# Attention scores from 64-row products in both halves of the array, four heads to a softmax step

## The chip, the cores and the metric

One core of a Trainium2 chip runs the whole program. The metric is the device time of one execution in microseconds. Five engines take their own instruction queues: TensorE (PE, and PEld for its loads of weights), VectorE (DVE), ScalarE (ACT), GpSimd (POOL) and SyncE (SP), which only issues DMAs here.

## The reference

Two networks run one after the other on 256 rows of 1024 features. The first is a block with stick-breaking attention, a recurrence and a feed-forward part. The second has two layers of attention and a product-key expert layer. The change is in the attention of the second, and each layer computes there, with h the running activations:

```python
proj = h @ w_in[l]                      # 8 + 8 query heads, 2 + 2 key/value heads, 64 wide
qa = apply_axial_rope(rms_norm_2(qa, qn_g[l]), cos, sin)
ka = apply_axial_rope(rms_norm_2(ka, kn_g[l]), cos, sin)
oa = global_attention(qa, ka, va)       # softmax(q k / 8) v, 4 query heads to a key head
ob = window_sink_attention(qb, kb, vb, sink[l], slopes)
oa = rms_norm_2(oa, gn_a_g[l]...)       # each head by itself
ob = rms_norm_2(ob, gn_b_g[l]...)
mix = concat([oa, ob]) @ w_o[l]
h = layer_norm(ALPHA * h + mix, ln1_g[l], ln1_b[l])
h = layer_norm(ALPHA * h + peer_ffn(h, ...), ln2_g[l], ln2_b[l])
```

The windowed heads subtract a slope times the distance from the scores, leave out keys more than 128 away, and add a learned sink to the softmax's denominator. Everything is in fp32.

## The kernel before

`body` runs the first block, then for each of two layers `attention` and `peer`. All of it is written with a tile framework whose planner decides the order on each engine: it takes instructions by their place in the program, with those marked as high priority first, and by a timeline that it computes for itself. Engines take their instructions in that fixed order and wait for semaphores. Tiles of one tag share a given number of buffers, and a new tile waits until an old one was read for the last time. PSUM has eight banks of 512 fp32 columns in each partition.

`attention` first projects the input, in products of split fp32 weights, into queries and keys. The second key head of each kind stands in partitions 64 to 127 and the first in 0 to 63, and so do the queries that go with them: `qT[which][:, j]` holds head j of either key head, one in each half of the partitions. `which` is 0 for the global heads and 1 for the windowed ones. The keys `KB[which]` have 2 x 256 columns: 256 for each key head, with zeros in the other head's partitions (lines 1165 to 1168, filled by lines 1189 and 1220). So one product of 128 rows and 512 columns gives the scores of two heads at once (line 1239). In fp32 each product runs as two passes, and each pass is an own record of a weight load and a matmul.

The steps that follow run over 16 combinations in a layer: two halves t of the rows (128 queries each), two kinds `which`, four j; a step has two heads. In `attend` (line 1236) a step makes its scores in PSUM (`s`, three buffers of a bank), adds the slopes by two bf16 products for windowed heads (1241), takes the minimum of the negated scores (1245) and for windowed heads the sink (1248), then two exponentials on ScalarE that also sum (1250), corrects and inverts the sum (1252 to 1255), transposes the weights in four 128 x 128 pieces (1259) into the one buffer `pt`, copies them to SBUF (VectorE for global heads, 1264, ScalarE for windowed ones, 1262), multiplies by the values into the one buffer `o` (1268) and scales (1269). After each second step `norm` (1272) normalizes the four heads of a pair of j: a square, a sum, GpSimd's power (line 173), three products, and `transpose_split` (lines 371 to 373) through the one buffer `tr`. `out` (1295) multiplies them with the output weights (1304), into two banks that collect a half t. `load` (1292) brings these weights in during the first eight steps: ScalarE rounds them (221) and GpSimd subtracts (222). The loop over n at line 1319 sets the order: a step's norm comes one step after its pair is complete, its products with the output weights two steps after.

When the last product of a half is there, `residual` and `finish` (1307, 1311) add, normalize the rows and transpose them into `X`, which `peer` needs for its first product. `K.warm` fills the wait with products that nobody reads, in a buffer of `s`. PSUM in this stage: two banks for `out`, three for `s`, one each for `pt`, `o` and `tr`. `peer` takes over all but the first two. Weights stream in through three buffers `raw`, so DMAs for the next stage start when a buffer is free.

Of the kernel before, what the change touches and what calls it, by code (L numbers as in the profile page):

```python
# [8 lines left out]
F = mybir.dt.float32  # L9
# [10 lines left out]
S = 256  # L20
# [1099 lines left out]
def attention(tc, A, K, dump, h, l, X, B):  # L1120
# [5 lines left out]
    with ExitStack() as es:  # L1126
# [38 lines left out]
        KB = [at.tile([128, 2, S], F, name=f"KB{i}") for i in range(2)]  # L1165
        for x in KB:
            G.memset(x[64:128, 0], 0.0)
            G.memset(x[0:64, 1], 0.0)
# [15 lines left out]
        def evb(j, ps):  # L1184
            if j < 4:
                V.tensor_scalar_mul(qT[1][:, j], ps, -0.125)
            else:
                for kv in range(2):
                    SC.activation(KB[1][64 * kv:64 * kv + 64, kv], ps[64 * kv:64 * kv + 64], AF.Copy)

# [25 lines left out]
        for t in range(2):  # L1216
            w = K.bank()
            PE.transpose(w[:, 0:128], RP[:, t, 4].rearrange("p k d -> p (k d)"), ident)
            for kv in range(2):
                SC.activation(KB[0][64 * kv:64 * kv + 64, kv, ts(t)], w[64 * kv:64 * kv + 64, 0:128], AF.Copy)  # L1220
            w = K.bank()
            for j in range(4):
                PE.transpose(w[:, j * 128:(j + 1) * 128], RP[:, t, j].rearrange("p k d -> p (k d)"), ident)
            V.tensor_scalar_mul(qT[0][:, :, ts(t)], w.rearrange("p (j t) -> p j t", t=128), -0.125)
# [11 lines left out]
        def attend(which, t, j):  # L1236

            s = pb.tile([128, 2, S], F, name="s", tag="s", bufs=3)
            PE.matmul(s, lhsT=qT[which][:, j, ts(t)], rhs=KB[which], start=True, stop=not which)
            for kv in range(2 * which):  # L1240
                PE.matmul(s[:, kv], lhsT=slope[:, j + 4 * kv], rhs=db[:, t], start=False, stop=kv == 1)
            mn = at.tile([128, 2], F, name="mn", tag="mn", bufs=4)
            dn = at.tile([128, 2], F, name="dn", tag="dn", bufs=4)
            P = at.tile([128, 2, S], F, name="P", tag="P", bufs=3)
            V.tensor_reduce(mn, s, AX.X, OP.min)
            sk = nsink.rearrange("p (k j) -> p k j", k=2)[:, :, j]
            if which:
                V.tensor_tensor(mn, mn, sk, op=OP.min)
            for kv in range(2):
                SC.activation(P[:, kv], s[:, kv], AF.Exp, scale=-1.0, bias=mn[:, kv:kv + 1], accum_out=dn[:, kv:kv + 1])  # L1250
            if which:
                V.tensor_sub(mn, mn, sk)
                SC.activation(mn, mn, AF.Exp)
                V.tensor_add(dn, dn, mn)
            V.reciprocal(dn, dn)
            w = pb.tile([128, 512], F, name="pt", tag="pt").rearrange("p (a t) -> p a t", t=128)
            for kv in range(2):
                for i in range(2):
                    PE.transpose(w[:, 2 * kv + i], P[:, kv, ts(i)], ident)
            PT = at.tile([128, 4, 128], F, name="PT", tag="PT", bufs=2)  # L1260
            if which:
                SC.activation(PT, w, AF.Copy)
            else:
                V.tensor_copy(PT, w)
            o = pb.tile([128, 512], F, name="o", tag="o")
            for kv in range(2):
                for i in range(2):
                    PE.matmul(o[:, kv * 64:kv * 64 + 64], lhsT=PT[:, 2 * kv + i], rhs=VA[:, i, which, 64 * kv:64 * kv + 64], start=i == 0, stop=i == 1)  # L1268
            V.tensor_mul(O[:, t, 8 * which:8 * which + 8].rearrange("p (k j) d -> p k j d", k=2)[:, :, j],
                         o[:, 0:128].rearrange("p (k x) -> p k x", x=64), dn.unsqueeze(2).to_broadcast([128, 2, 64]))  # L1270

        def norm(which, t, a):
# [14 lines left out]
            K.transpose_split(lambda: pb.tile([128, 512], F, name="tr", tag="tr"), sq, OH[:, ks, ts(t)], OL[:, ks, ts(t)])  # L1287
# [23 lines left out]
        def finish(t):  # L1311
            K.layer_norm(h, t, lambda c: g1[:, c], lambda c: b1[:, c])
            K.transpose_split(K.bank if t else lambda: pb.tile([128, 512], F, name="tr", tag="tr"), h[:, t].rearrange("p (m k) -> p k m", k=8),
                              *[x[:, :, ts(t)] for x in X])

        X = K.xt()
        steps = [(which, t, j) for t in range(2) for which in range(2) for j in range(4)]
        order = [0, 2, 1, 3, 4, 6, 5, 7]
        for n in range(19):
            if n < 16:  # L1320
                attend(*steps[n])
                if n < 8:
                    load(order[n])
            if n > 1 and n % 2 == 0 and n <= 16:
                which, t, j = steps[n - 1]
                norm(which, t, j // 2)
            if n > 2 and n % 2 == 1 and n <= 17:
                which, t, j = steps[n - 2]
                out(which, t, j // 2)
                if n == 9:  # L1330
                    residual(0)
        w = pb.tile([128, 512], F, name="s", tag="s", bufs=3)[:, :S]
# [321 lines left out]
```

## Time and profile before

| | us |
|---|---|
| median of 3 runs (2461.76 to 2466.64) | 2463.34 |
| the profiled execution | 2460.61 |
| its span | 2458.8 |

| engine | busy, share of the span | instructions |
|---|---|---|
| PE | 95% | 17012 |
| DVE | 69% | 3190 |
| ACT | 49% | 2118 |
| POOL | 15% | 299 |

The mean granted TensorE clock is 0.982 of full speed. Busy times are shares over stages with different limits, and matmuls overlap in the records, so a stage has to be looked at by itself: by its windows, its chain of waits and its groups of instructions. In the chain, each piece is what the next one waited for or followed on its engine.

### The profile page before, as it was taken

To read this page: it belongs to the slowest core of one execution; us is meant where nothing else is said; L and a number is where in the kernel's file an instruction comes from. 1 tells how busy PE (TensorE), PEld (TensorE's weight loads), DVE (VectorE), ACT (ScalarE), POOL (GpSimd) and SP (SyncE) were. 2 spreads that over 40 slices of the span, in tenths; PEclk is the share of its full clock that TensorE was granted. 3 is DMA by queue.
4 is the path that set the end of the run, shared out by engine and by line. 5 is a ranking of instruction groups with operands and counts; after the bars stand their busy time and mean duration, and the time that the engine had idled before them with its cause. 6 is when DMAs were issued, how large, how long until landed. Compare 5 with 4: busy or idle time off the path is not lost.

```text
span 2458.8 us, 43487 instructions
## 1 busy us (share of the span) xinstructions
PE 2346.7 (95%) x17012; PEld 2122.6 (86%) x17012; DVE 1697.5 (69%) x3190; ACT 1205.5 (49%) x2118; POOL 370.3 (15%) x299
## 2 busy tenths in 40 slices
PE   8978989998999999999999999999999999999998
PEld 7877879977799999999888877689999999888886
DVE  4467565557789968886555556779967888556555
ACT  4663554444435445544545454534545554455543
POOL 0065400007304410000000004502430000000000
PEclk9999999998999999999999999999999999999999
DMA  5332146555145454545556565325455555566664
GB/s 176 86 108 76 57 145 185 185 181 164 57 138 164 155 179 157 166 161 188 191 196 191 194 204 179 112 78 168 152 171 165 163 163 178 190 191 196 192 194 146
DMA packets 145637, 389.68 MB, mean 158 GB/s; under 512 B 18731, under 2 KB 49510, under 8 KB 145174
## 3 DMA queue, kind: packets, MB, share of 16 engines
q1 hardware_dynamic: 140070, 375.34, 47.8%
q10 hardware_dynamic: 5360, 11.56, 1.5%
q8 instruction: 133, 2.18, 0.4%
q14 instruction: 74, 0.61, 0.1%
HBM read 385.34 MB, written 1.31 MB: 157 GB/s over the span
## 4 chain that ended last, share of the span: by engine, by line
PE 56%; DVE 14%; issue 2%; ACT 2%; DMA 2%; POOL 0%; ACTq 0%; DVEq 0%; POOLq 0%
PE w L1571 27%; PE a L1387 7%; PE a L1388 7%; PE a L1390 7%; DVE lo L222 3%; PE w L1542 2%; PE a L1304 2%; DVE s L1434 1%; DMA raw<-in_peer_v_dram 1%; DVE oh L1469 1%; ACT hi L221 1%; PE w L1423 1%; PE o L1268 1%; DVE oh L1472 1%; DVE ix L1436 1%
## 5 line engine op out<-in xcount | busy, mean ns | idle before, releaser
L221 ACT ACTIVATE hi<-raw 128x1024 fp32r<-128x1024 f32 (+1 forms) x696 | 709.2, 1023 | 853.1 <-PE w L1571 312.0
L222 DVE TENSOR_TENSOR lo<-raw,hi 128x1024 fp32r<-128x1024 f32 (+1 forms) x610 | 745.7, 1224 | 524.6 <-ACT hi L221 518.9
L1387 PE MATMUL a<-XH,hi 128*128 128x256 f32 x2048 | 505.8, 285 | 8.9 <-ACT S L1393 5.9
L1388 PE MATMUL a<-XL,hi 128*128 128x256 f32 x2048 | 499.9, 282 | 0.0
L1571 PE MATMUL w<-hi,ww 128*128 128x512 f32 x1968 | 488.9, 389 | 4.1 <-ACT ww L226 4.1
L1571 PEld LDWEIGHTS w<-hi,ww 128*128 128x128 f32 x1968 | 368.8, 188 | 83.0 <-ACT ww L226 6.6
L1387 PEld LDWEIGHTS a<-XH,hi 128*128 128x128 f32 x2048 | 391.3, 191 | 12.7 <-ACT S L1393 6.3
L1388 PEld LDWEIGHTS a<-XL,hi 128*128 128x128 f32 x2048 | 391.3, 191 | 0.0
L1390 PE MATMUL a<-XH,lo 128*128 128x256 f32 x2048 | 293.2, 284 | 8.3 <-DVE lo L222 8.3
L1390 PEld LDWEIGHTS a<-XH,lo 128*128 128x128 f32 x2048 | 262.8, 190 | 9.3 <-DVE lo L222 9.1
L1571 PE MATMUL w<-lo,ww 128*128 128x512 f32 x984 | 264.4, 390 | 0.0
L222 POOL TENSOR_TENSOR lo<-raw,hi 128x1024 fp32r<-128x1024 f32 (+1 forms) x86 | 190.6, 2226 | 314.0 <-ACT hi L221 289.1
L173 POOL TENSOR_TENSOR ag<-ag,mhalf 128x1 f32<-128x1 f32 x10 | 9.5, 951 | 1464.0 <-DVE ag L349 1253.0
L1571 PEld LDWEIGHTS w<-lo,ww 128*128 128x128 f32 x984 | 184.2, 188 | 40.3 <-DVE lo L222 2.3
L264 PE MATMUL pj<-XH,hi 128*128 128x256 f32 (+1 forms) x424 | 124.6, 299 | 5.1 <-ACT gs L593 3.3
L266 PE MATMUL pj<-XH,lo 128*128 128x256 f32 (+1 forms) x424 | 117.5, 300 | 4.9 <-DVE lo L222 3.8
L265 PE MATMUL pj<-XL,hi 128*128 128x256 f32 (+1 forms) x424 | 122.1, 293 | 0.0
L227 DVE TENSOR_TENSOR ww<-S,ww 128x256 fp32r<-128x256 f32 x246 | 102.5, 417 | 0.0
L226 ACT ACTIVATE ww<-S 128x256 fp32r<-128x256 f32 x246 | 98.0, 399 | 0.0
L265 PE MATMUL pj<-big,hi 128*128 128x256 f32 x352 | 97.8, 283 | 0.0
L264 PE MATMUL pj<-big,hi 128*128 128x256 f32 x352 | 97.4, 283 | 0.0
L266 PE MATMUL pj<-big,lo 128*128 128x256 f32 x352 | 92.6, 283 | 0.0
(502 smaller groups left out, 3564.3 us busy)
## 6 DMA issues: line engine op xcount, KB each, us to landing
raw<-in_peer_u_dram SPq DMA_DIRECT2D x256, 512.0 KB
raw<-in_peer_v_dram SPq DMA_DIRECT2D x256, 512.0 KB
raw<-in_w_in_dram SPq DMA_DIRECT2D x58, 512.0 KB
raw<-in_w_ffn_in_dram SPq DMA_DIRECT2D x88, 256.0 KB
raw<-in_peer_wq_dram SPq DMA_DIRECT2D x32, 512.0 KB
raw<-in_w_ffn_out_dram SPq DMA_DIRECT2D x22, 512.0 KB
raw<-in_w_o_dram SPq DMA_DIRECT2D x16, 512.0 KB
raw<-in_w_out_dram SPq DMA_DIRECT2D x8, 512.0 KB
```

The costliest lines, as they stand in the source:

```text
L221: nc.scalar.activation(a, r, AF.Copy)
L222: (sub or nc.vector).tensor_sub(b, r, a.bitcast(F))
L226: self.nc.scalar.activation(hi, xf, AF.Copy)
L227: self.nc.vector.tensor_sub(lo, xf, hi.bitcast(F))
L264: PE.matmul(ps[j], lhsT=wh, rhs=xh(kk), start=kk == 0 and j % per == 0, stop=False)
L265: PE.matmul(ps[j], lhsT=wh, rhs=xl(kk), start=False, stop=False)
L266: PE.matmul(ps[j], lhsT=wl, rhs=xh(kk), start=False, stop=kk == KT - 1 and (j % per == per - 1 or j == len(subs) - 1))
L1304: K.marks["out"] = PE.matmul(po[t][c], lhsT=x[:, k, ts(t)], rhs=w[:, c * 512:(c + 1) * 512], start=f and not i and k == ks[0], stop=e and ...
L1387: PE.matmul(a, lhsT=hi[:, k], rhs=XH[:, k], start=k == 0, stop=False)
L1388: PE.matmul(a, lhsT=hi[:, k], rhs=XL[:, k], start=False, stop=False)
L1390: PE.matmul(a, lhsT=lo[:, k], rhs=XH[:, k], start=False, stop=k == 7)
L1571: K.marks["v"] = PE.matmul(acc[t][:, n], lhsT=x[:, ts(t)], rhs=v[:, n * 512:(n + 1) * 512], start=f, stop=e)
```

## The change

Keys lose their zeros: `KB[which]` has 256 columns, both key heads one above the other, and is filled by one copy in place of two. `attend` takes two j at once, four heads: four score products of 64 rows and 256 columns, each with the queries and keys of one half of the partitions, into a tile `s` of two banks (one for each key head) with two buffers. Minimum, sink, correction, inversion and scaling then work on four heads in one instruction; exponentials, transposes, copies and value products stay as many as they were. The copy of the transposed weights is VectorE's for the first j and ScalarE's for the second, whatever the kind of heads. `norm` and `finish` take their transposes from `pt`, and `tr` is gone. The loop has nine turns: `attend` of a pair, then `norm` and `out` of the pair before.

```diff
-        KB = [at.tile([128, 2, S], F, name=f"KB{i}") for i in range(2)]
-        for x in KB:
-            G.memset(x[64:128, 0], 0.0)
-            G.memset(x[0:64, 1], 0.0)
+        KB = [at.tile([128, S], F, name=f"KB{i}") for i in range(2)]
...
-                for kv in range(2):
-                    SC.activation(KB[1][64 * kv:64 * kv + 64, kv], ps[64 * kv:64 * kv + 64], AF.Copy)
+                SC.activation(KB[1], ps, AF.Copy)
...
-            for kv in range(2):
-                SC.activation(KB[0][64 * kv:64 * kv + 64, kv, ts(t)], w[64 * kv:64 * kv + 64, 0:128], AF.Copy)
+            SC.activation(KB[0][:, ts(t)], w[:, 0:128], AF.Copy)
...
-        def attend(which, t, j):
-
-            s = pb.tile([128, 2, S], F, name="s", tag="s", bufs=3)
-            PE.matmul(s, lhsT=qT[which][:, j, ts(t)], rhs=KB[which], start=True, stop=not which)
-            for kv in range(2 * which):
-                PE.matmul(s[:, kv], lhsT=slope[:, j + 4 * kv], rhs=db[:, t], start=False, stop=kv == 1)
...
-            P = at.tile([128, 2, S], F, name="P", tag="P", bufs=3)
+        def attend(which, t, a):
+
+
+            s = pb.tile([128, 2, 2, S], F, name="s", tag="s", bufs=2)
+            for j in range(2):
+                for kv in range(2):
+                    r = slice(64 * kv, 64 * kv + 64)
+                    PE.matmul(s[:, kv, j], lhsT=qT[which][r, 2 * a + j, ts(t)], rhs=KB[which][r], start=not j, stop=j == 1 and not which)
+            for j in range(2 * which):
+                for kv in range(2):
+                    PE.matmul(s[:, kv, j], lhsT=slope[:, 2 * a + j + 4 * kv], rhs=db[:, t], start=False, stop=j == 1)
...
+            P = at.tile([128, 2, 2, S], F, name="P", tag="P", bufs=2)
             V.tensor_reduce(mn, s, AX.X, OP.min)
...
-            PT = at.tile([128, 4, 128], F, name="PT", tag="PT", bufs=2)
-            if which:
-                SC.activation(PT, w, AF.Copy)
-            else:
-                V.tensor_copy(PT, w)
...
+            o = pb.tile([128, 512], F, name="o", tag="o")[:, 0:256].rearrange("p (k j d) -> p k j d", k=2, j=2)
+            for j in range(2):
+                w = pb.tile([128, 512], F, name="pt", tag="pt").rearrange("p (a t) -> p a t", t=128)
+                for kv in range(2):
+                    for i in range(2):
+                        PE.transpose(w[:, 2 * kv + i], P[:, kv, j, ts(i)], ident)
+                PT = at.tile([128, 4, 128], F, name="PT", tag="PT", bufs=2)
+                if j:
+                    SC.activation(PT, w, AF.Copy)
+                else:
+                    V.tensor_copy(PT, w)
+                for kv in range(2):
+                    for i in range(2):
+                        PE.matmul(o[:, kv, j], lhsT=PT[:, 2 * kv + i], rhs=VA[:, i, which, 64 * kv:64 * kv + 64], start=i == 0, stop=i == 1)
+            V.tensor_mul(O[:, t, 8 * which:8 * which + 8].rearrange("p (k j) d -> p k j d", k=2)[:, :, 2 * a:2 * a + 2],
+                         o, dn.unsqueeze(3).to_broadcast([128, 2, 2, 64]))
...
-            K.transpose_split(lambda: pb.tile([128, 512], F, name="tr", tag="tr"), sq, OH[:, ks, ts(t)], OL[:, ks, ts(t)])
+            K.transpose_split(lambda: pb.tile([128, 512], F, name="tr", tag="pt"), sq, OH[:, ks, ts(t)], OL[:, ks, ts(t)])
...
-        for n in range(19):
-            if n < 16:
+        for n in range(9):
+            if n < 8:
                 attend(*steps[n])
-                if n < 8:
-                    load(order[n])
-            if n > 1 and n % 2 == 0 and n <= 16:
-                which, t, j = steps[n - 1]
-                norm(which, t, j // 2)
-            if n > 2 and n % 2 == 1 and n <= 17:
-                which, t, j = steps[n - 2]
-                out(which, t, j // 2)
-                if n == 9:
+                if n < 4:
+                    load(order[2 * n])
+                    load(order[2 * n + 1])
+            if n:
+                norm(*steps[n - 1])
+                out(*steps[n - 1])
+                if n == 4:
                     residual(0)
```

## Rows read from the trace of the kernel before

**Rows 1.** The page's first part: busy us (share of the span) and instructions.

```profile
PE 2346.7 (95%) x17012; PEld 2122.6 (86%) x17012; DVE 1697.5 (69%) x3190; ACT 1205.5 (49%) x2118; POOL 370.3 (15%) x299
```

**Rows 2.** Windows view: start and end, length, each engine's busy us, granted clock, DMA.

```profile
606.00:675.00 69.00, 63.47 (x355) 47.02 (x356) 48.73 (x143) 36.59 (x112) 24.30 (x21) 1.00 0.21 70
614.70:628.00 13.30, 11.67 (x68) 7.50 (x67) 13.22 (x36) 11.71 (x35) 9.95 (x9) 1.00 0.47 156
...
1561.60:1573.20 11.60, 9.50 (x60) 6.36 (x58) 11.43 (x27) 9.12 (x26) 10.04 (x9) 1.00 0.53 171
```

**Rows 3.** Chain of waits in the first layer's stage: shares, then start, us, what.

```profile
by line: PE a L1304 27.1%; PE o L1268 13.4%; PE s L1239 10.4%; PE pt L1259 7.8%; DVE mn L1245 6.5%; DVE sq L1283 2.8%; DVE PT L1264 2.6%; PE tr L371 2.6%; DVE mn L1248 2.5%; issue 2.3%; DVE h L1309 1.9%; ACT L1250 1.9%; DVE bs L346 1.7%; DV
...
606.18 0.28 ACT KB L1220
...
606.55 1.11 PE s L1239 x2
...
607.68 0.70 DVE mn L1245
...
621.25 0.07 DVE dn L1254
...
629.57 0.86 PE s L1239 x2
```

**Rows 4.** Chain of waits in the second layer's stage.

```profile
by line: PE a L1304 26.9%; PE o L1268 11.6%; PE s L1239 8.6%; ACT P L1250 7.3%; PE pt L1259 5.8%; issue 3.6%; DVE mn L1245 3.6%; PE tr L371 3.1%; DVE dn L1254 2.9%; ACT big L221 2.2%; DVE sq L1283 2.2%; DVE h L1309 1.8%; ACT L1250 1.8%; DVE
...
1551.03 1.70 PE s L1239 x2
```

**Rows 5.** Groups by line and form, 606 to 675 us: busy us, mean ns, idle before.

```profile
L373 DVE TENSOR_TENSOR big<-tr,big 128x256 fp32r<-128x256 f32 x8 | 3.4, 421 | 3.2 <-ACT big L372 3.2
...
L372 ACT ACTIVATE big<-tr 128x256 fp32r<-128x256 f32 x8 | 3.1, 383 | 13.4 <-PE tr L371 13.4
L1248 DVE TENSOR_TENSOR mn<-mn,nsink 128x2 f32<-128x2 f32 x8 | 2.5, 315 | 0.1
...
L1252 DVE TENSOR_TENSOR mn<-mn,nsink 128x2 f32<-128x2 f32 x8 | 1.9, 238 | 0.6 <-ACT P L1250 0.5
```

**Rows 6.** TensorE in order of time, products of 64 columns in either half.

```profile
120.71 0.66 PE L559 MATMUL w<-a,VS 128*64 128x256 f32 x4
121.19 0.39 PE L560 MATMUL w<-a,VS 128*64 128x128 f32 x4
...
283.15 0.32 PE L952 MATMUL pm<-QT,UU 128*64 128x128 f32 x1
283.15 0.32 PE L951 MATMUL pm<-RT,VN 128*64 128x128 f32 x1
283.31 0.27 PE L952 MATMUL pm<-QT,UU 128*64 128x128 f32 x1
```

**Rows 7.** TensorE in order of time, products of 64 rows between full ones.

```profile
206.16 1.02 PE L743 MATMUL pj<-ART,KZ 128*128 128x256 f32 x4
207.11 0.49 PE L786 MATMUL pm<-D 64*128 64x128 f32 x2
207.44 0.38 PE L787 MATMUL pm<-D 64*128 64x128 f32 x2
...
207.88 0.22 PE L790 MATMUL pm<-ident,D 64*128 64x64 f32 x1
208.03 0.71 PE L730 MATMUL pj<-VN,Nt 128*128 128x128 f32 x4
```

**Rows 8.** Groups by line and form, 1551 to 1621 us.

```profile
L1254 DVE TENSOR_TENSOR dn<-dn,mn 128x2 f32<-128x2 f32 x8 | 3.0, 373 | 1.0 <-ACT mn L1253 1.0
L1252 DVE TENSOR_TENSOR mn<-mn,nsink 128x2 f32<-128x2 f32 x8 | 2.7, 336 | 0.5 <-ACT P L1250 0.4
...
L1248 DVE TENSOR_TENSOR mn<-mn,nsink 128x2 f32<-128x2 f32 x8 | 2.4, 294 | 0.1
```

**Rows 9.** GpSimd in order of time.

```profile
616.17 2.54 POOL L222 TENSOR_TENSOR keep<-raw,keep 128x512 fp32r<-128x512 f32 x2
```

More of the change, by code (lines that the diff above doesn't have):

```diff
@@ L1255, in attend @@
             V.reciprocal(dn, dn)
[L1256 to L1259, printed above, removed]
-            PT = at.tile([128, 4, 128], F, name="PT", tag="PT", bufs=2)
-            if which:
-                SC.activation(PT, w, AF.Copy)
-            else:
-                V.tensor_copy(PT, w)
[L1265 to L1270, printed above, removed]
+            o = pb.tile([128, 512], F, name="o", tag="o")[:, 0:256].rearrange("p (k j d) -> p k j d", k=2, j=2)
+            for j in range(2):
+                w = pb.tile([128, 512], F, name="pt", tag="pt").rearrange("p (a t) -> p a t", t=128)
[7 more added lines that the diff above has]
+                    V.tensor_copy(PT, w)
+                for kv in range(2):
+                    for i in range(2):
+                        PE.matmul(o[:, kv, j], lhsT=PT[:, 2 * kv + i], rhs=VA[:, i, which, 64 * kv:64 * kv + 64], start=i == 0, stop=i == 1)
+            V.tensor_mul(O[:, t, 8 * which:8 * which + 8].rearrange("p (k j) d -> p k j d", k=2)[:, :, 2 * a:2 * a + 2],
+                         o, dn.unsqueeze(3).to_broadcast([128, 2, 2, 64]))
         def norm(which, t, a):
@@ L1312, in finish @@
             K.layer_norm(h, t, lambda c: g1[:, c], lambda c: b1[:, c])
-            K.transpose_split(K.bank if t else lambda: pb.tile([128, 512], F, name="tr", tag="tr"), h[:, t].rearrange("p (m k) -> p k m", k=8),
+            K.transpose_split(K.bank if t else lambda: pb.tile([128, 512], F, name="tr", tag="pt"), h[:, t].rearrange("p (m k) -> p k m", k=8),
                               *[x[:, :, ts(t)] for x in X])
         X = K.xt()
-        steps = [(which, t, j) for t in range(2) for which in range(2) for j in range(4)]
+        steps = [(which, t, a) for t in range(2) for which in range(2) for a in range(2)]
         order = [0, 2, 1, 3, 4, 6, 5, 7]
-        for n in range(19):
-            if n < 16:
+        for n in range(9):
+            if n < 8:
                 attend(*steps[n])
-                if n < 8:
-                    load(order[n])
-            if n > 1 and n % 2 == 0 and n <= 16:
-                which, t, j = steps[n - 1]
-                norm(which, t, j // 2)
-            if n > 2 and n % 2 == 1 and n <= 17:
-                which, t, j = steps[n - 2]
-                out(which, t, j // 2)
-                if n == 9:
+                if n < 4:
[5 more added lines that the diff above has]
+                if n == 4:
                     residual(0)
-        w = pb.tile([128, 512], F, name="s", tag="s", bufs=3)[:, :S]
+        w = pb.tile([128, 2, 2, S], F, name="s", tag="s", bufs=2)[:, 0, 0]
         K.warm(48, "out", w)
```

9 lines of the change are left out of this document (4 added, 5 removed).

## The prediction

> **What bounds the kernel now.** I read the page's line of engine totals first: TensorE's matmul records cover 95% of the span [rows 1]. That is an average, so the next view is the stage that the diff touches: the attention of each of the two layers, from the first scores to the last product with the output weights, 606 to 675 us and 1551 to 1621 us. In the first of them TensorE is busy 63.5 of 69 us and VectorE 48.7 [rows 2]. The chain of waits, read in order of time, then shows that the stage has three parts. It starts as one dependent line: the second of two key copies, one score step, VectorE's minimum over the scores [rows 3], a table load on ScalarE, the first exponentials. Then comes a stretch in which VectorE is full: 13.22 of 13.3 us from 614.7 to 628.0, and 11.43 of 11.6 us in the second layer, while TensorE in the same stretches has 1.6 and 2.1 us free [rows 2]. From there to the end the chain is mostly TensorE. Nothing after the stage can begin before it ends, since the next stage takes its operand from the layer norm behind it; DMA issues ahead stop at three buffers. So what the stage loses, the kernel loses, twice.
>
> **The products.** A score step today is one product of 128 rows and 512 columns, in two passes: 0.86 us of stream for a step [rows 3]. Two steps cost 1.72 us. After the change a pair of steps is four products of 64 rows and 256 columns, eight records. A pass over 256 columns takes half of 0.43, 0.215 us, so one after another they would again be 1.72; if the halves run at the same time, four passes remain, 0.86 us.
> No row shows two row halves at once. The nearest is the output of the first block, where 64 output columns go to either half of the array: four records of 256 columns start at 120.71 and the next line's start at 121.19, so they took 0.48 us, not 0.86. A later pair of lines shows how: both start at 283.15, one in each half, before the first one's second pass at 283.31 [rows 6]. I take full overlap from these rows.
> Working with half the array has a price, seen where 64-row products stand between full ones. Four records of 256 columns begin at 206.16 and should end their stream at 207.02, but the first half-array product begins at 207.11: 0.09 lost. Its two records take 0.33 us where the following ones take 0.11 each, since the first load of weights was not hidden: 0.11. On the way back, the last one (64 columns) starts at 207.88, its stream ends by 207.94, and the next begins at 208.03: 0.09 [rows 7]; its first load, too, can't have been hidden, 0.11 as on the way in. Together 0.40 us for a pair. So a pair costs 0.86 + 0.40 = 1.26 in place of 1.72: 0.46 less. The bounds are 0.39 more (no overlap, 2.11) and 0.86 less (no price of switching).
> How much of it counts is read in the chain. In the first layer 10.4% of 69 us, 7.2, are scores: 1.11 at the start and seven later steps like the one at 629.57. In the second 8.6% of 70, 6.0: 1.70 at the start, where a step takes twice its usual time, and five later steps [rows 3, 4]. Twelve later steps are six pairs: 6 x 0.46 = 2.8 us. The pairs at the start fill time in which TensorE waits for exponentials anyway.
>
> **VectorE.** Each of its small operations on the row statistics takes 0.07 us on the chain [rows 3], and a reduction of 1024 in place of twice 512 spares one such fixed part. The windowed heads need six operations of a step (minimum, comparison with the sink, difference, sum, reciprocal, scaling), so a pair drops six: 0.42; the other heads' three give 0.21. The full stretch holds mainly the four windowed steps of the first row half, two pairs: 0.84 us in each layer.
> A second part is larger. The sink operations last 0.15 us when undisturbed, but on average 0.315 and 0.238 in the first layer, 0.294, 0.336 and 0.373 in the second, eight of each [rows 5, 8]. They do so while GpSimd subtracts halves of the output weights, 1.27 us each [rows 9]: an operation that reads two SBUF operands seems to wait for it. The excess sums to 8 x (0.165 + 0.088) = 2.0 us and 8 x (0.144 + 0.186 + 0.223) = 4.4 us. With half as many operations I take half: 1.0 and 2.2. Bounds: none (each of fewer operations waits longer) and all of it.
> Against this, the copies of transposed weights, now VectorE's for the first heads and ScalarE's for the windowed ones, are split evenly. Their number stays, but one more falls into the full stretch, 0.6 us a layer: 1.2 back. VectorE's sum: 2 x 0.84 + 1.0 + 2.2 - 1.2 = 3.7 us. TensorE can follow, from its free time there and its own saving.
>
> **Smaller edits.** One key copy in place of two stands on the chain: 0.28 us less [rows 3]. The first minimum reads twice as much: from 0.42 us for 256 elements [rows 5] to its 0.70 for 512 [rows 3] an element costs 1.1 ns, so 512 more cost 0.56. Net 0.28 later, in both layers 0.6. At the slow start of the second layer the first pair's four short passes are as long as the one step's two now (1.70), so nothing is added. The four clears of keys stand on GpSimd ahead of the projections, and it is busy 15% of the span [rows 1]: nothing, and 0.3 us each if its next work were late.
> PSUM: scores take four banks in place of three, so the norm's transposes lose their own bank and share the one of the weights. A turn holds it for two transposes, ScalarE's 0.38 us and VectorE's 0.42 [rows 5], about 1.1 us with the transposes. The weights' own two turns (four transposes of 0.11 and a copy of 512 elements, 0.70) are about 1.2 each, together 3.5 us, and a pair has 63.5 / 8 = 7.9 us of TensorE work, so the bank fits if the order is good. I take 0.05 us a pair, 0.8 in all; bounds 0 and 16 x 1.1 = 18.
>
> **Sum.** 2.8 + 3.7 - 0.6 - 0.8 = 5.1 us less. The profiled execution took 2460.6 us around a span of 2458.8 and would take 2455.5. The median of the runs shown is 2463.3, 2.7 above; there the forecast is 2458.2.
>
> **Rivals.** First: the halves don't overlap. Then six pairs cost 0.39 more each, +2.3 in place of -2.8, and the time is 2463.3. For it: no row shows row halves. Against: the column halves.
> A milder form would be strict order among the products: the second half's first pass could start only with the first half's second, making five passes of four, 0.215 more a pair and 2459.5. The rows speak against it: the second line's first pass came at 283.15, not with the first line's second at 283.31 [rows 6]. [...]
> Second, on the slower side: the shared bank. TensorE takes its instructions in order, so a transposition that waits for the bank holds the scores and output products behind it. The gain is gone when each of the 16 pairs stalls by 0.05 + 5.1 / 16 = 0.37 us; if each waits once for a whole copy, 0.70, it is -5.1 - 0.8 + 11.2 = +5.3, or 2468.6. For it: VectorE and ScalarE are late in the full stretch, just where the bank must be emptied. Against: over 4 of a pair's 7.9 us don't need the bank.
> Third: more than forecast. All 16 pairs count (7.4), and VectorE's excess goes whole (1.7 + 6.4 - 1.2 = 6.9): less the two costs, 12.9. Two thirds of the way there from 5.1 are 10.3 less, 2453.0.
>
> **How the numbers follow.** Forecast 0.50, first rival 0.12 (a third of it the mild form), second 0.18, third 0.20. A measurement of this kernel tells about 0.2%, 4.9 us, from no change: under 2458.4 is faster, over 2468.2 slower by as much. The forecast's own range, 2454 to 2462, is parted near its middle, a little more of it below: 0.29 faster, 0.21 same. The third rival is faster, the first same. The second spreads around 2468.6, since the stall can be a part of a copy or more than one: 0.13 slower, 0.05 same. Faster 0.49, same 0.38, slower 0.13. The range, 2451 to 2467, leaves out most of the second rival and the end of the third.
>
> **What will show it.** Half-array score products should start in couples, 0.01 to 0.05 us apart, and a pair should take near 1.0 us from its first start to its last pass; 1.7 means the first rival. VectorE's count in the stage should fall by some 36 a layer and the sink operations' excess should halve. TensorE waits that end with the copy of the transposed weights or with the norm's subtraction, and that grow by more than 6 us together, mean the second. The forecast fails too if the schedule parts a pair's products, so that the 0.40 is paid twice.

## The result

The changed kernel is slower: 2501.96 us, median of four executions (2499.84 to 2506.39), against 2462.55 for the kernel before on the same chip, a ratio of 1.0169 with a 95% interval of 1.0156 to 1.0181. That is 39 us more, where 5 less were forecast, and outside the range of 2451 to 2467.

The profile after has a span of 2499.5 us and a mean granted clock of 0.978 (before: 0.982). Its page's first part, which answers to [rows 1]:

```profile
PE 2351.6 (94%) x17076; PEld 2128.8 (85%) x17076; DVE 1694.9 (68%) x3118; ACT 1199.8 (48%) x2104; POOL 368.9 (15%) x291
```

This line hardly differs from the one before. The windows of the two attention stages, from the first scores to the last product with the output weights, hold the whole loss (start and end, length, busy us of PE, PEld, DVE, ACT, POOL, granted clock, DMA share, GB/s). The kernel after:

```profile
606.30:696.30 90.00, 71.29 (x390) 54.37 (x391) 44.29 (x106) 34.45 (x106) 24.27 (x21) 0.87 0.17 54
1570.20:1663.20 93.00, 68.81 (x389) 53.59 (x390) 46.92 (x107) 34.52 (x106) 28.16 (x24) 0.89 0.18 57
...
615.00:636.00 21.00, 18.52 (x91) 13.36 (x90) 13.22 (x30) 11.03 (x31) 10.55 (x9) 0.70 0.46 150
```

The kernel before, cut at the same two events:

```profile
606.50:675.50 69.00, 63.97 (x358) 47.23 (x359) 49.11 (x142) 36.15 (x110) 23.80 (x21) 1.00 0.21 69
1551.00:1621.20 70.20, 65.62 (x358) 47.82 (x359) 51.19 (x142) 35.73 (x110) 25.23 (x23) 0.98 0.22 75
```

The stages grow by 21.0 and 22.8 us, 43.8 together; the spans differ by 40.7, so the rest of the kernel took a little less. Of the 43.8 us, growth of TensorE's time without work (length less busy) is 33.3: it was 5.0 and 4.6, and is 18.7 and 24.2. The other 10.5 are longer busy time, with less to compute: the granted clock was 1.00 and 0.98 and is 0.87 and 0.89. From 615 to 636 us of the kernel after it is 0.70 on average: 0.50 from 611 to 620 and from 628 to 634, 1.00 between them from 621 to 627. The same work takes longer there: the eight score records of a pair (L1238) that start at 617.51 us, at 0.50, take 2.08 us, and those at 621.95, at 1.00, take 1.14. In the run a_pts below, in ten us with a clock of 0.67 on average, the eight records of output products (L1270) that start at 617.49 us take 1.97 us, and those at 622.49 take 1.00.

What TensorE waited for, first layer (line, releaser: us in total, times, longest). The kernel before, then after:

```profile
PE s L1239 <- ACT KB L1220: 1.5, 1, 1.5
PE o L1268 <- DVE PT L1264: 1.4, 2, 1.0
PE pt L1259 <- ACT P L1250: 1.0, 1, 1.0
```

```profile
PE o L1270 <- DVE PT L1267: 5.2, 6, 1.3
PE tr L371 <- ACT PT L1265: 4.3, 6, 0.7
...
PE pt L1262 <- ACT P L1251: 2.4, 1, 2.4
...
PE o L1270 <- ACT PT L1265: 0.7, 1, 0.7
```

The waits that end with the copy of transposed weights are 10.2 us (5.2 + 4.3 + 0.7), where they were 1.4; in the second layer they are 11.1 (5.6 + 4.3 + 1.2), where they were 2.3. One pair on the chain of waits shows how (start, us, what); the kernel after:

```profile
652.04 1.14 PE s L1238 x8
...
653.72 2.78 PE a L1306 x12
656.50 0.45 PE pt L1262 x4
...
656.97 0.70 DVE PT L1267
...
657.72 1.11 PE o L1270 x8
658.82 0.46 PE pt L1262 x4
...
659.36 0.60 ACT PT L1265
659.96 1.82 ACT P L1251 x8
```

The transposes (L1262) fill the one bank; VectorE copies it, 0.70; the output products (L1270) follow; the second transposes fill the bank; ScalarE copies it, 0.60, and with ScalarE come the next pair's four exponentials (eight records, 1.82), which queue behind that copy. TensorE has nothing to put into these waits. In the kernel before, products with the output weights stood between the transposes and the output products:

```profile
656.46 0.44 PE pt L1259 x4
656.91 1.85 PE a L1304 x8
658.76 0.44 PE pt L1259 x4
659.20 0.84 PE o L1268 x8
```

### The profile page after: what moved, and what is told of

The parts are those of the page before. It is cut to its first block, busy times and chain, and to the rows that moved or that the text cites. A ratio compares the mean times of both kernels' runs of the same rounds, so it can differ in the third digit from the quotient of the medians.

```text
span 2499.5 us, 43505 instructions
## 1 busy us (share of the span) xinstructions
PE 2351.6 (94%) x17076; PEld 2128.8 (85%) x17076; DVE 1694.9 (68%) x3118; ACT 1199.8 (48%) x2104; POOL 368.9 (15%) x291
## 4 chain that ended last, share of the span: by engine, by line
PE 56%; DVE 13%; ACT 3%; issue 2%; DMA 2%; POOL 0%; DVEq 0%; ACTq 0%; POOLq 0%
PE w L1571 26%; PE a L1387 7%; PE a L1388 7%; PE a L1390 7%; DVE lo L222 3%; PE w L1542 2%; PE a L1306 2%; DMA raw<-in_peer_v_dram 1%; DVE s L1434 1%; PE w L1423 1%; ACT hi L221 1%; PE o L1270 1%; PE pj L302 1%; DVE oh L1469 1%; ACT P L1251 1%
```

## The experiments

All times are medians on a chip with runs of the kernel before beside them (2460 to 2463 us); ratios are to that kernel, with 95% intervals. Rows from different chips are better compared by their ratios where a few us matter.

| kernel | us | ratio | interval |
|---|---|---|---|
| after | 2502.0 | 1.0169 | 1.0156 to 1.0181 |
| b_share | 2534.2 | 1.0303 | 1.0282 to 1.0323 |
| a_lag | 2488.2 | 1.0106 | 1.0088 to 1.0125 |
| a_P3 | 2497.0 | 1.0142 | 1.0125 to 1.0159 |
| a_zeros | 2514.1 | 1.0208 | 1.0180 to 1.0235 |
| a_pts | 2480.3 | 1.0080 | 1.0054 to 1.0105 |
| a_pts_lag | 2484.7 | 1.0092 | 1.0075 to 1.0109 |
| a_pts_zeros | 2485.2 | 1.0103 | 1.0084 to 1.0121 |
| a_warm | 2494.9 | 1.0141 | 1.0124 to 1.0158 |
| a_pts_warm | 2472.9 | 1.0041 | 1.0029 to 1.0054 |
| a_pts_steps | 2475.5 | 1.0057 | 1.0040 to 1.0073 |
| a_pts_first | 2474.7 | 1.0054 | 1.0037 to 1.0070 |
| a_pts_first_warm | 2471.8 | 1.0036 | 1.0022 to 1.0050 |
| a_ot | 2485.8 | 1.0090 | 1.0069 to 1.0110 |
| a_ot_steps | 2489.7 | 1.0111 | 1.0094 to 1.0128 |
| a_ot_warm | 2477.0 | 1.0068 | 1.0050 to 1.0086 |
| a_ot_steps_warm | 2488.1 | 1.0111 | 1.0093 to 1.0130 |
| a_pts_gate | 2476.2 | 1.0059 | 1.0047 to 1.0071 |
| a_pts_gate_warm | 2466.7 | 1.0016 | 1.0007 to 1.0025 |

### The shared bank by itself

b_share is the kernel before with one edit, the norm's transposes (and in the same way those of `finish`) in the bank of the transposed weights:

```
- K.transpose_split(lambda: pb.tile([128, 512], F, name="tr", tag="tr"), sq, ...)
+ K.transpose_split(lambda: pb.tile([128, 512], F, name="tr", tag="pt"), sq, ...)
```

> The kernel before, with one edit: the norm's and the first half's transposes take the bank of the transposed weights, as in the change; the loop, the steps of two heads and the 128-row products stay. If sharing the bank is by itself the cause, each of 16 norms stalls TensorE by one copy or more and most of the 39.4 us come back here: 2480 to 2502. If the cause is the order in which the shared bank is handed round together with output products that come right behind the norm, the old loop with its step of delay still has work to put between, and this stays within 8 us of before: 2462 to 2471.

It costs 74 us, 4.6 for each of 16 pairs: more than the whole change. Its largest wait in the first layer (0.2 us in the kernel before), and its chain between two pairs:

```profile
PE tr L371 <- DVE sq L1285: 18.4, 6, 5.6
```

```profile
657.06 1.02 POOL rn L173
...
658.10 0.49 DVE sq L1283 x2
658.59 0.60 DVE mn L1245
659.19 0.33 DVE sq L1285
...
659.67 0.42 PE tr L371 x2
...
660.12 0.39 ACT big L372
```

In a shared bank the norm's transposes have a turn among those of the weights, and the next weights can't be transposed before that turn is over. So the norm's chain (GpSimd's power, 1.02 us; VectorE's products; the transposes; ScalarE's copy), which ran beside other work, now stands between successive weights. The 74 us are not all waiting: the clock fell here too. The first layer's stage:

```profile
607.80:711.50 103.70, 75.60 (x358) 54.29 (x359) 51.64 (x143) 36.68 (x110) 22.83 (x21) 0.87 0.13 46
```

With as many products as before, TensorE is busy 75.60 us here and 74.77 in the second layer, 20.8 more together; the two stages grew by 67.5.

### Softening it in the kernel after

a_lag lets the output projection follow one turn later; a_P3 gives the weights before transposition three buffers in place of two:

```
-            if n:
-                norm(*steps[n - 1])
-                out(*steps[n - 1])
+            if 1 <= n <= 8:
+                norm(*steps[n - 1])
+            if n > 1:
+                out(*steps[n - 2])
```

```
- P = at.tile([128, 2, 2, S], F, name="P", tag="P", bufs=2)
+ P = at.tile([128, 2, 2, S], F, name="P", tag="P", bufs=3)
```

> The changed kernel with the output products of a pair one turn later, behind the norm of the next pair, as the loop before had it by one step more; bank sharing, pairs, buffers and 64-row products stay. If TensorE waits because nothing is left to put between a transposition and the product that needs its copy, the waits on copies (4 to 5 us for each of the two kinds in the first layer) mostly go, and with them the stretches at half clock: 2465 to 2482. If the buffers or the shared bank set the pace whatever the order, it stays at 2495 to 2505.

> The changed kernel with a third buffer for the exponentials of a pair. If the loop is closed by the two buffers (the exponentials of a pair wait for the transposes of the pair two before, and the scores behind them hold the queue of TensorE), the wait of the scores for exponentials (0.5 to 0.7 us a pair, 2 us a layer) goes and pairs overlap again: 2475 to 2490. If these buffers are merely late and not the bound, 2495 to 2503.

a_lag gives back 14 us, between its two expectations; a_P3 about 5, within its second expectation, its interval touching that of the kernel after. The waits of a_lag in the first layer say why:

```profile
PE tr L371 <- ACT PT L1265: 4.3, 6, 0.7
...
PE o L1270 <- DVE PT L1267: 0.9, 2, 0.5
```

With a pair's projection in hand TensorE fills the wait for VectorE's copy (5.2 us to 0.9). The wait of the norm's transposes for ScalarE to empty the bank stays at 4.3: that one is made by the bank's turns.

### The products

a_zeros takes the 64-row products back inside the kernel after (128 rows, zeros in the keys, and with them the clears and the double key copies); a_pts_zeros does so where no bank is shared (next section):

```
+ for x in KB:
+     G.memset(x[64:128, 0], 0.0)
+     G.memset(x[0:64, 1], 0.0)
- PE.matmul(s[:, kv, j], lhsT=qT[which][r, 2 * a + j, ts(t)], rhs=KB[which][r], ...)
+ PE.matmul(s[:, j], lhsT=qT[which][:, 2 * a + j, ts(t)], rhs=KB[which], ...)
```

> The changed kernel with the old products: keys with zeros, 128 rows by 512 columns, one for each j, in the same two banks and buffers; the rest is as changed. The prediction's price of the products is 0.46 us a pair in favour of 64 rows, so without them the time should be 3 to 8 us longer, 2505 to 2510. If switching the array between halves and whole costs more than the halves give, it is shorter than 2500; if the lower clock comes from the thinner products, shorter by 10 or more.

> The kernel with the weights transposed into the score banks and the norm's own bank, but its products again of 128 rows with zeros in the keys, as before the change. It tells what 64-row products are worth where the stage does not wait for the shared bank. Forecast's step: 6 pairs x 0.46 = 2.8 us over the two layers, so 2 to 5 us above the run with 64-row products. Rival (the products are worth as much as in the kernel after, where taking them back cost 12 us): 9 to 15 us above.

By the medians the old products cost 12 us more in the kernel after, above what was expected (the intervals touch), and 5 where no bank is shared, as the forecast's step has it (the intervals overlap). So the products are most probably a gain, and nothing here says that they caused the loss. They count more in the kernel after, I think, because part of its stage runs at a clock of 0.50, where a pair's score records take 2.08 us in place of 1.14; that was not tried apart.

64-row products alone, in the steps of the kernel before, where both heads of a step lie in one bank, were not tried; no run shows what they would give there. In this kernel the gain came with scores of four banks.

### A bank of its own for the norm

In a_pts the transposed weights go into the pair's own two score banks, after the exponentials have read them, and the norm has its bank back; a_pts_lag adds the later projection.

```
- w = pb.tile([128, 512], F, name="pt", tag="pt").rearrange("p (a t) -> p a t", t=128)
+ w = s[:, j].rearrange("p a (b t) -> p (a b) t", t=128)
- K.transpose_split(lambda: pb.tile([128, 512], F, name="tr", tag="pt"), sq, ...)
+ K.transpose_split(lambda: pb.tile([128, 512], F, name="tr", tag="tr"), sq, ...)
```

> The kernel after, but the transposed weights are written into the pair's own two score banks once the exponentials have read them, and the transposes of the norm have a bank of their own again. Theory (the loss comes from the norm's transposes taking turns with the weights' in one bank): the 39 us go, and what is left is the gain that was forecast for the products and VectorE; 2445 to 2465 us, the attention stage at 66 to 70 us in both layers, TensorE without a half-clock stretch of over 4 us. Rival (pairs themselves are too coarse a step: the exponentials of a pair, 1.8 us, hold the copies and so TensorE): 2480 to 2500 us, with the waits on ScalarE's copy and the half-clock stretches still there.

> As the run before (weights transposed into the score banks, the norm with its own bank), and the output projection of a pair moved one turn later, in a loop of ten turns. Theory: with its own bank the norm is in time, so the later projection changes little, within 6 us of the run before (2445 to 2465). Rival (the chain through square, power and products is late for the projection even with its own bank): 8 us or more below the run before.

22 of the 39 us go, and a later projection adds nothing any more. But 20 us are left. The time misses the theory's range and lies at the lower edge of the rival's (pairs are too coarse a step), and the rival's signs are there too: stretches at a lower clock, 0.67 to 0.78 in three of the windows below, and a wait of 3.2 us for ScalarE's copy. The windows of a_pts:

```profile
606.30:682.60 76.30, 65.40 (x389) 53.48 (x390) 42.80 (x106) 35.77 (x106) 23.30 (x21) 0.89 0.20 63
...
606.00:616.00 10.00, 5.13 (x30) 4.20 (x31) 3.64 (x6) 8.53 (x25) 7.61 (x7) 0.78 0.54 165
616.00:626.00 10.00, 7.50 (x40) 6.04 (x38) 4.34 (x8) 5.07 (x8) 7.93 (x7) 0.67 0.63 207
626.00:636.00 10.00, 9.11 (x45) 7.17 (x46) 5.58 (x17) 5.13 (x20) 1.01 (x1) 0.69 0.36 108
636.00:646.00 10.00, 10.00 (x70) 8.46 (x68) 6.04 (x17) 4.73 (x17) 1.01 (x1) 1.00 0.01 2
```

From 636 to 646 us TensorE is full and at full clock. What is left is mostly in the first 30 us: less to do, 5.13 and 7.50 of 10, and a clock of 0.67 to 0.78. Its two largest waits in the stage:

```profile
PE s L1262 <- ACT P L1251: 4.6, 2, 3.8
PE o L1270 <- ACT PT L1265: 3.2, 1, 3.2
```

The longest single one, 3.8 us, is for the first pair's weights, four exponentials and a minimum of 1024 elements away; before it was 1.0.

### The clock

a_warm puts six idle products, 0.11 us each (28 of them took 3.23 us in a_pts_gate_warm), behind each four transposes of the kernel after, with its order unchanged; a_pts_warm does so in the first row tile of a_pts only, with 32 more behind the first scores:

```
+ spare = o[:, 256:512]
+ K.marks["pt"] = PE.transpose(w[:, 2 * kv + i], P[:, kv, j, ts(i)], ident)
+ K.warm(6, "pt", spare)
```

> The kernel after with its order and its one bank, and six products of the identity (128 columns of weights, 256 columns, 2 bytes) behind the four transposes of the weights of each step, into columns of the output bank that nobody reads: TensorE works where it would wait for the copy. 192 products are added, some 0.11 us each at the full clock, 20 us in all, of which what lies in the waits costs nothing. Theory A (the waits alone make the loss, the clock is a small part of it): half-clock stretches shrink but the time stays or rises, 2498 to 2515 us. Theory B (the lower clock makes half of the loss: 20 to 24 us of each layer's stage were at half clock in the kernel after, so up to 10 to 12 us a layer of doubled durations): 2478 to 2494 us, with the half-clock stretches below 8 us a layer.

> The kernel with the weights transposed into the score banks, and fillers for TensorE at the start of each attention stage: 32 products of the identity (2 bytes, 256 columns) behind the first pair's scores, six behind each four transposes of the weights of the first row tile, into columns that nobody reads. Fillers lie where TensorE waited (3.8 us for the first pair's weights, 10.7 and 11.9 us a stage in all). Theory S (what is left of the loss with the own bank, 17 to 20 us, is the start of the stage: the first pair comes later, and TensorE then runs 17 us at half clock in each layer): half-clock stretches fall under 7 us a layer and 8 to 14 us go, 2464 to 2472 us. Rival (the late start is a matter of ScalarE's and VectorE's queues, and TensorE's clock only goes with it): less than 4 us go, or the fillers cost.

a_warm gains 7 us, just short of theory B, although it adds some 20 us of work; its stages have a granted clock of 0.94 and 0.96. a_pts_warm gains 7 by the medians and 10 by the ratios (1.0080 to 1.0041), where 8 to 14 were expected, with a clock of 1.00 through both stages; the first:

```profile
607.20:681.60 74.40, 68.25 (x470) 55.63 (x471) 43.23 (x106) 35.44 (x106) 24.20 (x21) 1.00 0.20 65
```

Both intervals just touch those of the kernels without fillers. So the clock probably costs some 10 us in a_pts, but 10 more stay.

### The start, and the shared softmax step

a_pts_first halves the first pair's minimum and sends its first transposes to an idle bank; a_pts_first_warm adds fillers; a_pts_steps does minimum, sink, reciprocal, copies, output and division step by step as before the change, with 64-row products as in a_pts.

```
+ for x in range(2) if first else [slice(0, 2)]:
+     V.tensor_reduce(mn[:, :, x], s[:, :, x], AX.X, OP.min)
```

> As the run with the weights in the score banks, but the first pair of each stage takes its minimum in two halves and its first transposes go to an idle bank, so that the first exponentials and the first transposes start as early as with single steps: minimum 0.70 us in place of 1.24, transposes behind two exponentials in place of three (0.45 us). Theory S: the first transposes come 1 us sooner in each layer, and if that keeps TensorE at its full clock, up to 6 us a layer more; 2466 to 2479 us. Rival: 1 us a layer at most, 2478 to 2481 us.

> The two runs before together: first pair in halves, 20 fillers behind the first scores and six behind the transposes of the first row tile. Theory S: both gains add, 2460 to 2470 us, at best no slower than the kernel before the change. Rival: as the run with the first pair in halves, within 4 us.

> As the run with the weights in the score banks, but softmax, copies, products and division again step by step, as before the change: two minima, two reciprocals, two divisions and two output tiles a pair. It takes back the shared softmax step alone, where no bank is shared. Forecast's step: the shared softmax saves 3.7 us on VectorE in the two layers, so 2482 to 2488 us. Rival (the shared step hurts, since the first exponentials wait for a minimum twice as long and the weights come in one burst): 2466 to 2476 us.

2474.7, 2471.8 and 2475.5 us: each 5 to 8 below a_pts (2480.3), the first and third with overlapping intervals. The gains of first pair and fillers don't add. The shared softmax step, taken back, is not 4 us slower but by the median 5 faster, as the rival has it: in this arrangement its saving doesn't reach the time.

### Output and norm in one bank

Here the weights have a bank of their own, and output (columns 0 to 255) and norm (256 to 511) share one. a_ot is this alone; a_ot_steps takes the shared softmax step back, and the two others add 48 fillers a layer.

```
+ ob = pb.tile([128, 512], F, name="o")
- o = pb.tile([128, 512], F, name="o", tag="o")[:, 0:256].rearrange(...)
+ o = ob[:, 0:256].rearrange(...)
- K.transpose_split(lambda: pb.tile([128, 512], F, name="tr", tag="pt"), sq, ...)
+ K.transpose_split(lambda: ob[:, 256:512], sq, ...)
```

> The kernel after, but the norm's transposes go to the unused half of the output's bank (columns 256 to 511; the output of a pair takes 0 to 255), so that nothing shares the bank of the transposed weights, which stays a bank of its own. Theory (the turns in the shared bank make about 20 us, the late first pair and its half clock some 10 us, and 8 to 10 us come from the weights' transposes holding the score banks in the runs that put them there): 2465 to 2478 us, below every run without fillers so far. Rival (what is left is the pair as a step, whatever bank): 2476 to 2486 us, like the run with the weights in the score banks (2480).

> As the run before (output and norm's transposes in two halves of one bank), with softmax, copies, products and division step by step again; only the 64-row products of two steps stay together. It takes the shared softmax step back where banks do not matter. Forecast's step: the shared step saves 3.7 us, so 2 to 5 us above the run before. Rival (the shared step costs, by later first exponentials): 3 to 8 us below the run before, and then 2460 to 2472 us.

> As the run with output and norm's transposes in one bank, with 24 fillers (products of the identity, 0.11 us each) behind the first pair's scores and six behind each four transposes of the weights of the first two pairs, in each layer: 48 fillers, 5 us, for TensorE's waits at the start. Theory: half clock disappears at the start, 6 to 12 us below the run without fillers, 2456 to 2468 us. Rival: less than 3 us.

> 64-row products with softmax step by step, no bank shared with the transposed weights, and the fillers at the start: all that the runs so far found against the changed kernel is undone, and the products' gain is kept. If the account is full, it is at or below the kernel before the change: 2450 to 2462 us. If a cause is still missing, 2465 us or more.

a_ot gives 16 of the 39 us back, no more than a_pts, and lies in the rival's range: the theory that the score banks were held too long falls. Fillers gain 9 here. Steps in place of the shared softmax come out 4 us slower, as forecast, where they were 5 faster in a_pts, each time with overlapping intervals, so the shared step's worth is below what these runs can tell. The last run, meant to undo all, missed by over 20 us, so in this arrangement a cause is missing. Two halves of a bank may not have done as two banks here: in the first layer of a_ot the norm's transposes wait twice, 0.8 us in all, for the division that reads the other half. Nothing separates that from other effects of this order.

### The order on ScalarE

In the trace of a_pts ScalarE stands before the second copy of transposed weights like this (bracket: idle before, releaser):

```profile
622.37 1.06 ACT L221 ACTIVATE hi<-raw 128x1024 fp32r<-128x1024 f32 x1 [1.32 <-DMA raw<-in_peer_wq_dram]
625.08 1.06 ACT L221 ACTIVATE hi<-raw 128x1024 fp32r<-128x1024 f32 x1 [1.66 <-DMA raw<-in_peer_wq_dram]
626.04 0.58 ACT L1265 ACTIVATE PT<-s 128x512 f32<-128x512 f32 x1
```

Two roundings of the next stage's weights, each waiting for its DMA, are queued ahead of the copy that TensorE needs. (ScalarE waits 1.32 and 1.66 us for them; the 4.44 us of the expectation below are the DMA's own piece in the chain of waits.) a_pts_gate holds them behind the fourth pair's exponentials; a_pts_gate_warm adds 52 fillers a layer.

```
- hi, lo = K.load_split(src, 1024)
+ with K.behind(*["exp101"] * (not hd)):
+     hi, lo = K.load_split(src, 1024)
```

> As the run with the weights in the score banks, but the first two pieces of the next stage's weights (the query weights of the experts) are fetched and rounded on ScalarE only behind the fourth pair's exponentials. In the trace of that run ScalarE waits 4.44 us in layer 1 for the DMA of such a piece, with the copy of the transposed weights, and so TensorE, queued behind it. Theory Q (this queue order is a cause of its own): 4 us a layer go, more with the clock, 2468 to 2475 us. Rival (the wait only covers what VectorE and GpSimd hold back anyway): 2478 to 2483 us, as before.

> The same with fillers for TensorE's first waits: 28 behind the first pair's scores and six behind each four transposes of the weights of the first two pairs, 52 a layer in place of 68 or more in the run with fillers at 2473 us. If queue order and clock are the rest of the loss: 2456 to 2465 us, level with the kernel before. If the pair as a step is what is left: 2468 us or more.

a_pts_gate is 4 us below a_pts, between its two expectations, intervals overlapping: probable, not shown. With the fillers it is 2466.7 us, 10 lower with intervals apart. That is the clock again: TensorE's busy time in the two stages is 63.6 and 65.3 us in a_pts_gate, and 65.2 and 64.8 in a_pts_gate_warm with 5.7 us of fillers in each (52 of 0.11), so the kernel's own products take 10.3 us less, about what the time gains.

The kernel after has this queue order too. In the second layer of its trace one wait of TensorE for the norm's products lasts 5.6 us (first line; 0.3 at most in the kernel before), and the chain of waits runs there through a DMA for the next stage's weights and VectorE's subtraction of them:

```profile
PE tr L371 <- DVE sq L1287: 6.7, 2, 5.6
```

```profile
1586.14 3.50 DMA raw<-in_peer_wq_dram
...
1590.75 1.35 DVE lo L222
...
1595.79 0.68 PE tr L371 x2
```

So not all of that layer's 22.8 us are the shared bank; the gate was not tried in the kernel after.

a_pts_gate_warm lies between its two expectations. It is the fastest with the change in it, 4 us above the kernel before by the ratio (1.0007 to 1.0025), and none beat that kernel. Most of what is left is in the first layer (a stage of 72.3 us against 69.0, and 70.9 against 70.2 in the second). It shows when both are cut at the first product with the output weights. The windows of the kernel before, then of a_pts_gate_warm:

```profile
606.50:629.90 23.40, 20.65 (x111) 12.94 (x111) 19.81 (x49) 20.11 (x59) 16.69 (x14) 1.00 0.52 173
629.90:675.50 45.60, 43.32 (x250) 34.29 (x249) 29.30 (x93) 16.04 (x52) 7.11 (x8) 1.00 0.05 16
```

```profile
608.60:628.70 20.10, 17.74 (x147) 14.42 (x147) 9.27 (x21) 14.64 (x41) 15.58 (x14) 1.00 0.53 171
628.70:680.90 52.20, 47.44 (x296) 38.59 (x297) 33.50 (x86) 20.43 (x65) 7.64 (x8) 1.00 0.07 21
```

And TensorE's groups of scores and outputs in the first of the two windows, before and then a_pts_gate_warm (records, busy us, mean ns, idle before):

```profile
L1239 PE MATMUL s<-KB,qT 128*128 128x512 f32 x24 | 12.0, 596 | 1.5 <-ACT KB L1220 1.5
L1268 PE MATMUL o<-VA,PT 128*128 128x64 f32 x48 | 6.4, 276 | 1.7 <-DVE PT L1264 1.0 <-DVE rn L156 0.7
```

```profile
L1238 PE MATMUL s<-KB,qT 64*128 64x256 f32 x32 | 4.5, 402 | 1.2 <-ACT KB L1215 1.2
L1277 PE MATMUL o<-VA,PT 128*128 128x64 f32 x32 | 4.2, 275 | 1.5 <-ACT PT L1272 0.9 <-DVE PT L1274 0.6
```

By then the kernel before had the scores of 12 steps (24 records, two a step) and the output of 6 (48 records, eight a step); the changed one the scores of 8 steps (32 records, eight a pair) and the output of 4, and 5.7 us of its first 20.1 are fillers. It comes there 3.3 us sooner and has 6.6 us more to go. The time that its products save lies at the start, where TensorE has no other work, and the steps that it is behind come later. What holds the start back (the banks for two pairs of scores, the two buffers of weights, or the order) stays open.

## Why the prediction was wrong

**The shared bank** is the step that failed: 0.05 us a pair, 0.8 in all, bounded by 18, with no row behind the 0.05. Alone in the kernel before it costs 74 us; a bank of its own gives 22 of the changed kernel's 39 back, and part of that is the clock: with as many records, 779, TensorE is busy for 140.1 us in the two stages of the kernel after and for 131.8 in those of a_pts. The working counted how long the bank is held, 3.5 of 7.9 us, and found room. What b_share's trace shows to decide is the order of turns: the bank goes to the norm's late transposes before the next weights, and a chain that ran beside other work becomes a link between pairs. In the kernel after most of these waits end with the copies instead, since nothing stands between a copy and the product that needs it; a_lag, which changes only that order, gives 14 us back with the bank still shared. The upper bound counted one hold of 1.1 us a pair; it left out all that TensorE must do without meanwhile.

**The second rival** named this mechanism and its sign. Its test was a growth of over 6 us in the waits that end with the copy of the weights or with the norm's subtraction: the copy's alone went from 1.4 to 10.2 us in the first layer. Its price, one copy of 0.70 a pair, 11.2 in all, was too small: there are 13 such waits in each layer's eight pairs, 21.3 us together where 3.7 were, the next pair's exponentials queue behind the copy, and the clock falls to 0.87 and 0.89.

**The clock** was in no step. Every duration came from the kernel before, where the stage ran at full clock, 1.00 [rows 2]. How much it is can be read from a_pts_gate_warm, which has the same products at full clock throughout: TensorE is busy for 17.74 + 47.44 = 65.2 us in the first layer, less 5.7 of fillers 59.5. In the kernel after it is 71.3, so some 12 us of busy time in that layer are the lower clock; in the second layer, by 68.8 against 64.8 less 5.7, some 10.

**The products** were right in kind and undersized. Their records start in couples, as foreseen; the records that had started by 606.33 us:

```profile
606.32 0.49 PE L1238 MATMUL s<-KB,qT 64*128 64x256 f32 x2 [1.16 <-DVE qT L1219]
```

Two records start within 0.01 us. The row doesn't say which halves they are, but a pair's eight records took 1.14 us on the chain, where one after another they would take 1.72; 1.26 were forecast. By that the price of working with half the array is 0.28, not 0.40. So the first rival and its mild form, in which the first pass stands alone, fall. TensorE's own work fell by 64.0 - 59.5 = 4.5 us in the first layer, near 8 x 0.58 = 4.6: the saving covers all eight pairs, not the three and a half that the forecast counted in this layer. It is work saved, not time.

**VectorE** did as said: 142 to 106 instructions, 49.1 to 44.3 us of the first stage. The sink operations' excess over 0.15 us fell from 2.0 to 0.5 us in the first layer and from 4.4 to 2.6 in the second, by half in all, as forecast (here one group of the first layer, which answers to the 2.5 us of L1248 in [rows 5]):

```profile
L1248 DVE TENSOR_TENSOR mn<-mn,nsink 128x4 f32<-128x4 f32 x4 | 1.1, 267 | 0.0
```

But its 3.7 us were to come from the chain, and VectorE is no longer what the start waits for. No run shows them in the time.

**The start** was priced at 0.6 us, as a longer minimum less a key copy. The wait for the first weights went from 1.0 to 2.4 us in the kernel after, and in a_pts to 3.8, and the lower clock came behind it.

## What to carry to other kernels

A PSUM bank that two chains share must be judged by whose turn comes next and how late that one is, not by how long it is held (here 3.5 of 7.9 us, and the sharing alone cost 74): write out the order of turns and ask what TensorE has to do in each. Before a change that makes steps coarser, count the work that TensorE can do before the first step is through; where TensorE has no other work, less work on it is no gain (here 4.5 us less in the first layer didn't reach the time), and a longer pause can be followed by a lower clock (here pauses of 2.4 and 3.8 us were, by stretches at 0.67 to 0.78). A saving that comes with more banks has to be priced with them (here four for the scores in place of three).

## What the runs showed of the hardware

In the kernel before, waits of 1.5 and 1.0 us for the first keys and weights left TensorE at its full clock in the first layer, 1.00; in its second layer, with a wait of 2.1 us for the first keys, the clock was 0.98; waits of 2.4 us (the kernel after) and 3.8 (a_pts) were followed by stretches at 0.67 to 0.78 on average; in the kernel after it was 0.50 from 611 to 620 and from 628 to 634 us and 1.00 from 621 to 627. With products that nobody reads in those waits it was 1.00 through both stages of a_pts_warm and a_pts_gate_warm. Such fillers took 7, 7, 9 and 10 us off four kernels by the medians, the last one with intervals well apart, and 3 and 2 off two others, where the intervals overlap. The eight records of a pair's 64-row products start in four couples, within 0.01 us each (kernel after, from 606.32, 621.95 and 652.04 us), and a pair's four products of 64 rows take 1.14 us where two of 128 rows with zeros took 1.72, 0.86 each.
